# Row-wise L1 normalisation of 16,384 rows: all transfers on SyncE's one queue, in runs of two stores and two loads

## The chip, the core and the metric

The kernel runs on one core of a Trainium2 chip. The time is the device time of one execution in microseconds. Before the change it is 316.64 us (median of 3 runs, 316.48 to 316.65). One further execution was recorded by the hardware profiler. Everything that is said below about single instructions, transfers and packets comes from that execution.

Names used: DVE is VectorE, ACT is ScalarE, SP is SyncE, POOL is GpSimd. "ACTq" and "SPq" are the sequencers of ACT and SP, which issue transfers and wait for semaphores. A transfer is carried out by the core's 16 DMA engines, which are not the same thing as the engines that issue it.

## What is computed

```python
x = np.random.randn(32, 512, 1024).astype(np.float32)
sums = np.sum(np.abs(x), axis=-1, keepdims=True)
out  = (x / (sums + 1e-8)).astype(np.float32)
```

There are 16,384 independent rows of 1,024 fp32 numbers, 4 KB each. Every row is divided by the sum of its absolute values. Input and output are 67.11 MB each, so 134.22 MB have to be moved between HBM and SBUF, and each byte takes part in only two passes over it.

## The kernel before

**Tiling.** A tile is 128 partitions by up to 12 rows of 1,024 numbers, 6,144 KB in all, 49,152 bytes in each partition. There are 128 rows for each partition, cut into eleven tiles: tiles 0 to 9 have 12 rows, tile 10 has 8 (32,768 bytes in each partition). Within a tile each partition holds consecutive rows of HBM, so what one partition loads or stores of a whole tile is one contiguous piece of HBM. Four buffers of a tile's size (`BUFS = 4`) are used in turn: tile i+4 is loaded into the buffer of tile i, and can be loaded only when the store of tile i has landed.

**Compute of one tile** (`normalize`, lines 45 to 73). DVE reduces the whole tile to one sum of absolute values per row (L47, 12.95 us for 12 rows), adds the small constant (L54), takes the reciprocal (L56), and multiplies rows in place by their reciprocal in one broadcast multiply (L58, 12.96 us for 12 rows). For the first three and the last two tiles a few rows are taken from that multiply: `kt` rows are multiplied one by one on DVE (L65, 749 ns a row), `ks` rows on ACT (L68, 1,138 ns a row). The dictionary `split` holds the pairs (kt, ks).

**Order.** The order of instructions is written out by hand in a plain loop: first the loads of tiles 0 to 3, then for every tile its compute, its store, and the load of the tile four further on.

**Queues.** Loads are issued by SP (L87), stores by ACT (L97). So there are two DMA queues, and while both have work the 16 DMA engines serve them side by side: q1 in the profile carries the loads, q10 the stores. ACT also runs the L68 rows, in program order with the stores.

**Packets.** The argument `max_dma_last_dim` cuts what each partition moves into pieces of at most that many bytes, and each piece becomes one packet of the DMA engines. Loads of tiles 0 and 1 and stores of tiles 9 and 10 go whole, one packet per partition. All other loads, and the stores of tiles 1 to 8, go in pieces of 24,576 bytes (16,384 for the load of tile 10), two per partition. The store of tile 0 goes as two transfers, three rows in pieces of 4,096 bytes and nine rows whole; the store of tile 8 goes as two transfers of six rows. That makes 11 loads and 13 stores.

Of the kernel before, what the change touches and what calls it, by code (L numbers as in the profile page):

```python
# [1 line left out]

# [4 lines left out]

FP32 = mybir.dt.float32
EPS = 1e-8


@with_exitstack
def kernel(
    ctx: ExitStack,
    tc: tile.TileContext,
    x: bass.AP,
    out: bass.AP,
):
    nc = tc.nc
    P = nc.NUM_PARTITIONS  # L20

    x_flat = x.flatten_outer_dims()
    out_flat = out.flatten_outer_dims()
    n, d = x_flat.shape

    R = 12
    BUFS = 4
    HEAD = 32
    per_partition = n // P
    assert n % P == 0 and (per_partition - HEAD) % R == 0  # L30
    rows = [R] * ((per_partition - HEAD) // R + 2) + [HEAD - 2 * R]

    def piece(flat, i):
        head = flat[: P * HEAD, :].rearrange("(p r) d -> p r d", p=P)
        if i < 2:
            return head[:, R * i : R * (i + 1), :]
        if i == len(rows) - 1:
            return head[:, 2 * R :, :]
        a = P * (HEAD + R * (i - 2))
        return flat[a : a + P * R, :].rearrange("(p r) d -> p r d", p=P)  # L40

    sbuf = ctx.enter_context(tc.tile_pool(name="sbuf", bufs=BUFS))
    stats = ctx.enter_context(tc.tile_pool(name="stats", bufs=len(rows)))

    def normalize(x_tile, k, kv, kt):
        s = stats.tile([P, R], FP32)
        nc.vector.tensor_reduce(  # L47
            out=s[:, :k],
            in_=x_tile[:, :k, :],
            axis=mybir.AxisListType.X,  # L50
            op=mybir.AluOpType.add,
            apply_absolute_value=True,
        )
        nc.vector.tensor_scalar_add(out=s[:, :k], in0=s[:, :k], scalar1=EPS)  # L54
        inv = stats.tile([P, R], FP32)
        nc.vector.reciprocal(out=inv[:, :k], in_=s[:, :k])  # L56
        if kv:
            nc.vector.tensor_mul(  # L58
                out=x_tile[:, :kv, :],
                in0=x_tile[:, :kv, :],  # L60
                in1=inv[:, :kv].unsqueeze(2).to_broadcast([P, kv, d]),
            )
        for r in range(kv, kv + kt):
            row = x_tile[:, r, :]
            nc.vector.tensor_scalar_mul(out=row, in0=row, scalar1=inv[:, r : r + 1])  # L65
        for r in range(kv + kt, k):
            row = x_tile[:, r, :]
            nc.scalar.activation(  # L68
                out=row,
                in_=row,  # L70
                func=mybir.ActivationFunctionType.Copy,
                scale=inv[:, r : r + 1],
            )

    last = len(rows) - 1
    split = {0: (3, 4), 1: (0, 3), 2: (0, 3), last - 1: (0, 2), last: (4, 4)}

    tiles = {}

    HALF, WHOLE = 24576, 49152
    FIRST = 3

    def load(i):
        x_tile = tiles[i] = sbuf.tile([P, R, d], FP32, name="x_tile")
        nc.sync.dma_start(out=x_tile[:, : rows[i], :], in_=piece(x_flat, i), max_dma_last_dim=WHOLE if i < 2 else HALF)  # L87

    def store(i):
        if i == 0:  # L90
            parts = [(0, FIRST, 4 * d), (FIRST, R, WHOLE)]
        elif i == last - 2:
            parts = [(0, R // 2, HALF), (R // 2, R, HALF)]
        else:
            parts = [(0, rows[i], WHOLE if i >= last - 1 else HALF)]
        for a, b, size in parts:
            nc.scalar.dma_start(  # L97
                out=piece(out_flat, i)[:, a:b, :],
                in_=tiles[i][:, a:b, :],
                max_dma_last_dim=size,  # L100
            )

    def compute(i):
        k = rows[i]
        kt, ks = split.get(i, (0, 0))
        normalize(tiles[i], k, k - kt - ks, kt)

    with tc.manual_schedule():
        for i in range(BUFS):
            load(i)  # L110
        for i in range(len(rows)):
            compute(i)
            store(i)
            if i + BUFS < len(rows):
                load(i + BUFS)


# [1 line left out]
_INS = ['x']  # L119
_OUTS = [((32, 512, 1024), 'float32')]  # L120


# [23 lines left out]
```

## Time and profile before

| quantity | value |
|---|---|
| median time | 316.64 us |
| time of the profiled execution | 316.77 us |
| its span, first to last instruction | 315.2 us |
| DVE busy | 260.6 us (83% of the span) |
| ACT busy | 18.5 us (6%) |
| data moved | 134.22 MB, 426 GB/s over the span |
| DMA packets | 5,761, of which 385 are under 512 bytes |
| share of the 16 DMA engines' time: loads (q1), stores (q10) | 49.8%, 49.4% |

The span is shorter than the time by 1.57 us, which lies around the program's own instructions. The shares of the two queues are the summed durations of their packets, divided by 16 engines times the span. Of the packets under 512 bytes, 384 are the semaphore updates with which each of 24 transfers tells, once per DMA engine, that it has landed. TensorE has no part in this kernel.

In the profile, the idle time of DVE is 29.8 us, all of it ended by a load's landing: 17.8 us before the first tile, the rest in five waits of 1.4 to 2.7 us between 138 and 256 us.

### The profile page before, as it was taken

The numbers are of one execution on the slowest core, as the hardware profiler recorded it, in microseconds if no ns is written. First come the engines' busy times: TensorE is split into PE (matmuls) and PEld (weight loads), VectorE is DVE, ScalarE is ACT, GpSimd is POOL, SyncE is SP. The second block draws the span as 40 slices with busy tenths as digits, with TensorE's granted clock in tenths as the row PEclk, the third lists the DMA queues.
The fourth block names the chain that finished last, engine by engine and source line by source line (L and its number), as shares of the span: only waits on it lengthen the run. The fifth ranks groups of instructions, "written<-read, shape, count | busy, mean of one in ns | idle before, by whom it ended". The sixth has DMA issues, their size and how long they took to land.

```text
span 315.2 us, 172 instructions
## 1 busy us (share of the span) xinstructions
DVE 260.6 (83%) x50; ACT 18.5 (6%) x17; POOL 0.2 (0%) x4
## 2 busy tenths in 40 slices
DVE  0079999999999999989996997999699969999000
ACT  0010503004000000000000000000000000203200
POOL 0000000000000000000000000000000000000000
DMA  8999999999999999999999999999999999999997
GB/s 318 480 399 412 437 407 464 411 436 413 415 446 437 415 446 437 415 449 434 415 449 437 412 449 437 412 449 437 415 446 437 415 437 434 432 428 496 399 408 324
DMA packets 5761, 134.22 MB, mean 426 GB/s; under 512 B 385, under 2 KB 385, under 8 KB 769
## 3 DMA queue, kind: packets, MB, share of 16 engines
q1 hardware_dynamic: 2736, 67.11, 49.8%
q10 hardware_dynamic: 3024, 67.11, 49.4%
q14 instruction: 1, 0.00, 0.0%
HBM read 67.11 MB, written 67.11 MB: 426 GB/s over the span
## 4 chain that ended last, share of the span: by engine, by line
DVE 40%; DMA 33%; another core or an unknown queue 18%; ACT 1%; issue 0%; SPq 0%
DVE s L47 23%; DMA x_tile<-in_x_dram 17%; DMA out_dram<-x_tile 16%; DVE x_tile L58 15%; ACT x_tile L68 1%; DVE x_tile L65 1%; DVE inv L56 0%; DVE s L54 0%; SPq L87 0%
## 5 line engine op out<-in xcount | busy, mean ns | idle before, releaser
L47 DVE TENSOR_REDUCE s<-x_tile 128x12 f32<-128x12288 f32 (+1 forms) x11 | 138.2, 12562 | 29.8 <-DMA x_tile<-in_x_dram 29.8
L58 DVE TENSOR_TENSOR x_tile<-x_tile,inv 128x12288 f32<-128x12288 f32 (+3 forms) x10 | 113.6, 11358 | 0.5
L68 ACT ACTIVATE x_tile<-x_tile,inv 128x1024 f32<-128x1024 f32 x16 | 17.2, 1138 | 256.9 <-DVE inv L56 256.9
L65 DVE TENSOR_SCALAR x_tile<-x_tile,inv 128x1024 f32<-128x1024 f32 x7 | 4.8, 749 | 0.0
L56 DVE RECIPROCAL inv<-s 128x12 f32<-128x12 f32 (+1 forms) x11 | 2.5, 226 | 0.4
L68 ACT ACT_TABLE_LOAD x1 | 1.3, 1283 | 17.8 <-DMA x_tile<-in_x_dram 17.8
L54 DVE TENSOR_SCALAR s<-s 128x12 f32<-128x12 f32 (+1 forms) x11 | 1.9, 174 | 0.4
L130 POOL MEMSET const-bfloat16-1.0<- 128x1 bf16 x1 | 0.1, 101 | 0.0
L130 POOL MEMSET const-uint8-127<- 128x1 uint8 x1 | 0.1, 101 | 0.0
L130 POOL MEMSET const-float32-0.0<- 128x1 f32 x1 | 0.1, 98 | 0.2 <-issue 0.2
L130 POOL MEMSET const-float32-1.0<- 128x1 f32 x1 | 0.1, 98 | 0.0
## 6 DMA issues: line engine op xcount, KB each, us to landing
x_tile<-in_x_dram SPq DMA_DIRECT2D x10, 6144.0 KB, 36.9
out_dram<-x_tile ACTq DMA_DIRECT2D x8, 6144.0 KB, 49.1
out_dram<-x_tile ACTq DMA_DIRECT2D x2, 3072.0 KB, 33.4
out_dram<-x_tile ACTq DMA_DIRECT2D x1, 4608.0 KB, 37.9
x_tile<-in_x_dram SPq DMA_DIRECT2D x1, 4096.0 KB, 32.2
out_dram<-x_tile ACTq DMA_DIRECT2D x1, 4096.0 KB, 20.9
out_dram<-x_tile ACTq DMA_DIRECT2D x1, 1536.0 KB, 29.3
```

What stands on the lines that cost most here:

```text
L47: nc.vector.tensor_reduce(out=s[:, :k], in_=x_tile[:, :k, :], axis=mybir.AxisListType.X, op=mybir.AluOpType.add, apply_absolute_value=True,)
L54: nc.vector.tensor_scalar_add(out=s[:, :k], in0=s[:, :k], scalar1=EPS)
L56: nc.vector.reciprocal(out=inv[:, :k], in_=s[:, :k])
L58: nc.vector.tensor_mul(out=x_tile[:, :kv, :], in0=x_tile[:, :kv, :], in1=inv[:, :kv].unsqueeze(2).to_broadcast([P, kv, d]),)
L65: nc.vector.tensor_scalar_mul(out=row, in0=row, scalar1=inv[:, r : r + 1])
L68: nc.scalar.activation(out=row, in_=row, func=mybir.ActivationFunctionType.Copy, scale=inv[:, r : r + 1],)
L130: nc = _bacc.Bacc("TRN2", target_bir_lowering=False, num_devices=1)
```

## The change

All transfers are issued by SP, each as one transfer per tile without a limit on the piece: one packet of 49,152 bytes per partition for a 12-row tile, one of 32,768 bytes for the 8-row tile. The order on SP's queue becomes: loads 0 to 3; then stores 0 and 1, loads 4 and 5; stores 2 and 3, loads 6 and 7; stores 4 and 5, loads 8 and 9; stores 6 and 7, load 10; stores 8 and 9; store 10. There are 22 transfers in place of 24. ACT keeps the L68 rows and issues no transfer. The division of tile 10's rows changes from (4, 4) to (5, 3): five rows one by one on DVE, three on ACT. The tiles, the four buffers and the work on DVE are otherwise the same.

```diff
-    split = {0: (3, 4), 1: (0, 3), 2: (0, 3), last - 1: (0, 2), last: (4, 4)}
+    split = {0: (3, 4), 1: (0, 3), 2: (0, 3), last - 1: (0, 2), last: (5, 3)}
...
-    HALF, WHOLE = 24576, 49152
-    FIRST = 3
-
     def load(i):
         x_tile = tiles[i] = sbuf.tile([P, R, d], FP32, name="x_tile")
-        nc.sync.dma_start(out=x_tile[:, : rows[i], :], in_=piece(x_flat, i), max_dma_last_dim=WHOLE if i < 2 else HALF)
+        nc.sync.dma_start(out=x_tile[:, : rows[i], :], in_=piece(x_flat, i))
 
     def store(i):
-        if i == 0:
-            parts = [(0, FIRST, 4 * d), (FIRST, R, WHOLE)]
-        elif i == last - 2:
-            parts = [(0, R // 2, HALF), (R // 2, R, HALF)]
-        else:
-            parts = [(0, rows[i], WHOLE if i >= last - 1 else HALF)]
-        for a, b, size in parts:
-            nc.scalar.dma_start(
-                out=piece(out_flat, i)[:, a:b, :],
-                in_=tiles[i][:, a:b, :],
-                max_dma_last_dim=size,
-            )
+        nc.sync.dma_start(out=piece(out_flat, i), in_=tiles[i][:, : rows[i], :])
...
+    RUN = 2
     with tc.manual_schedule():
         for i in range(BUFS):
             load(i)
-        for i in range(len(rows)):
-            compute(i)
-            store(i)
-            if i + BUFS < len(rows):
-                load(i + BUFS)
+        for first in range(0, len(rows), RUN):
+            run = range(first, min(first + RUN, len(rows)))
+            for i in run:
+                compute(i)
+                store(i)
+            for i in run:
+                if i + BUFS < len(rows):
+                    load(i + BUFS)
```

## The prediction

> **What bounds the kernel now.** I read the page's busy shares and its 40 slices first, then the DMA queues, the chain of waits, the transfers' times to landing, and last the packets in chosen stretches. Busy shares, slices and queues:
>
> ```profile
> DVE 260.6 (83%) x50; ACT 18.5 (6%) x17; POOL 0.2 (0%) x4
> DVE  0079999999999999989996997999699969999000
> DMA  8999999999999999999999999999999999999997
> q1 hardware_dynamic: 2736, 67.11, 49.8%
> q10 hardware_dynamic: 3024, 67.11, 49.4%
> ```
>
> The 16 DMA engines are busy in every slice, DVE is not: it starts late, ends early and has dips. The two queues' shares add to 99.2% of 315.2 us, that is 312.7 us of packet time on each engine. So the end is set by the summed packet time, and idle time can be gained only at the two ends, about 2.5 us. The chain of waits, in its middle part:
>
> ```profile
> 111.34 48.94 DMA out_dram<-x_tile
> 160.28 0.02 issue
> ...
> 160.35 0.37 SPq L87
> 160.72 28.68 another core or an unknown queue
> 189.41 0.02 issue
> ...
> 189.48 0.37 SPq L87
> 189.84 28.59 another core or an unknown queue
> 218.43 0.02 issue
> ```
>
> The reader is to see the period. A store lands at 160.28, 189.41 and 218.43, and each landing frees a buffer for the next load: 29.08 us on average for one load and one store of a 12-row tile. Is that the speed of the DMA engines, or do the two directions hinder each other? Three stretches answer it; the columns of the queue lines are packets, MB, and share of 16 engines.
>
> Loads alone with 49,152-byte packets (3 to 31 us):
>
> ```profile
> q1 hardware_dynamic: 256, 11.80, 97.3%
> ```
>
> Loads and stores together with 24,576-byte packets (140 to 230 us):
>
> ```profile
> q1 hardware_dynamic: 841, 19.49, 50.3%
> q10 hardware_dynamic: 839, 19.44, 50.1%
> ```
>
> Stores alone with 32,768-byte packets (305 to 313 us):
>
> ```profile
> q10 hardware_dynamic: 105, 3.44, 99.5%
> ```
>
> In the first, 16 of the 256 are semaphore updates, so 240 packets took 0.973 x 28 x 16 = 435.9 us, or 1.816 us each. Each DMA engine carries 8 partitions, so a 12-row tile takes 8 x 1.816 = 14.5 us one way; two of them are 29.06 us, against 29.08 in the mixture. The third gives 0.995 x 8 x 16 / 105 = 1.213 us. The packet records themselves, sorted by size, have medians of 912 ns for 24,576 bytes, 1,815 for 49,152 and 1,213 for 32,768 in either direction, 609 for 16,384, 1,364 for 36,864 and 159 for 4,096. So each packet has some 9 ns that don't go with its bytes (2 x 912 - 1,815), neither direction is slower than the other, and mixing them costs next to nothing.
>
> **The change part by part.**
>
> *Packets.* On each DMA engine eight loads (tiles 2 to 9) and seven stores (1 to 7) go from 16 packets to 8, the 8-row load from 16 to 8, and the two halves of store 8, 16 together, become 8. That is 8 x (8 + 7 + 1 + 1) = 136 packets fewer. At 9 ns each this is 1.2 us. Store 0 now takes 8 x (3 x 159 + 1,364) ns = 14.73 us, whole 8 x 1,815 = 14.52: 0.2 us. Two transfers fewer save two semaphore updates of 9 ns, nothing. Sum: 1.4 us less packet time on each engine. The whole sum again, as a check: 20 transfers x 8 x 1.815 + 2 x 8 x 1.213 = 309.8 us, plus 22 updates (0.2) and the slow first packet (2.85 in place of 1.815, 1.04) = 311.0, against 312.7 before: 1.7 less, with 0.3 of rounding in the two shares. I take 1.4, the sum over single edits; the landings walked through below, last one at 312.7 against 314.2 before, give 1.5.
>
> *One queue, and SP's waits.* On SP a store now waits for compute, and every load behind it waits with it; a load waits for the landing of the store that frees its buffer, and the stores behind it wait too. None of this costs anything while the queue already holds undone transfers when the next one is issued. A dry queue has a price in the trace: the first load lands 17.0 us after its issue, 2.5 us over its 14.5 of data.
>
> ```profile
> x_tile<-in_x_dram SPq DMA_DIRECT2D x1, 6144.0 KB, 17.0
> ```
>
> So I walk through the order, first load landing at 17.8, then 14.5 us per 12-row transfer and 9.7 for the 8-row ones. Landings: L1 32.3, L2 46.8, L3 61.3, S0 75.8, S1 90.3, L4 104.8, L5 119.3, S2 133.8, S3 148.3, L6 162.8, L7 177.3, S4 191.8, S5 206.3, L8 220.8, L9 235.3, S6 249.8, S7 264.3, L10 274.0, S8 288.5, S9 303.0, S10 312.7. DVE's pass over a full tile is 12.95 (sum) + 0.2 + 0.3 + 12.96 = 26.3 us with gaps; with the splits 20.9 for tile 0, 23.1 for tiles 1 and 2, 24.3 for tile 9. The 8-row tile takes 8.69 + 0.4 + five L65 rows of 0.749 = 12.9 (three L68 rows of 1.138 end before that). The rows:
>
> ```profile
> L47 DVE TENSOR_REDUCE s<-x_tile 128x12 f32<-128x12288 f32 x10 | 129.5, 12949 | 29.8 <-DMA x_tile<-in_x_dram 29.8
> L58 DVE TENSOR_TENSOR x_tile<-x_tile,inv 128x12288 f32<-128x12288 f32 x6 | 77.8, 12959 | 0.4
> L47 DVE TENSOR_REDUCE s<-x_tile 128x8 f32<-128x8192 f32 x1 | 8.7, 8686 | 0.0
> L65 DVE TENSOR_SCALAR x_tile<-x_tile,inv 128x1024 f32<-128x1024 f32 x7 | 4.8, 749 | 0.0
> ```
>
> Compute then ends at 38.7, 61.8, 84.9, 111.2, 137.6, 163.9, 190.3, 216.6 for tiles 0 to 7 without a gap on DVE (each load has landed by then), 247.1 for tile 8 (3.7 us of waiting for L8, in place of the five waits before), 271.4 for tile 9 and 286.9 for tile 10 (waiting for L10, 274.0). Now each issue against the time at which the queue would run dry: S0 38.8 against 60.9; S1 61.9 against 75.4; L4 at S0's landing, 75.9, against 89.9; L5 90.4 against 104.4; S2 90.8 and S3 111.3 against 119 and 133; S4 after L7, 148.8, against 177; S5 164 against 191; S6 after L9, 206.8, against 235; S7 216.7 against 249; L10 249.9 against 264; S8 250.3 against 274; S9 271.5 against 288; S10 287.0 against 302.6. The cover is never under 13 us, nearly one transfer. The waits cost 0. If the cover went, each dry place would cost about 2.5 us. SP's issue of a store (0.34 to 0.50 us on ACTq, loads 0.37) lies under the same cover.
>
> A rule of the Trainium skill speaks against so strict an order (page "DMA: Bandwidth & Descriptors", section "Anatomy of one DMA"): each transfer carries a fixed cost of about 2.0 us besides its bytes, fitted on the other, software path. If a queue paid it for each of 22 transfers, 44 us would be added. By the trace's rows it is paid at the front of the first transfer alone: L1 (issued 1.15, 31.2 us to landing) lands 14.5 us after L0, which is packet time and nothing else.
>
> *Change of direction within one queue.* The order has nine: L3 to S0, S1 to L4, and so on. The trace shows none inside one queue. Low end 0: in the mixture each engine alternates direction at every packet, between the queues, and two tiles took 29.08 us against 29.06. High end: what the very first packet had over the others, 1.04 us each, 9.4 in all. Below nothing is excluded by the one-way stretches, which run at the same packet times. I take 0, the alternating row being nearest.
>
> *ACT, compute, the (5, 3) split.* Stores no longer stand between ACT's rows, and tile 10 ends at 286.9 with 15 us of cover. 0. Before the change the last store was issued at 293.25 with the store ahead of it landing at 304.5, so it was covered too.
>
> *Sum.* 316.77 - 1.4 = 315.4 us for a profiled execution. The median of the runs shown stands 0.13 under it, so 316.64 - 1.4 = 315.2.
>
> **The rivals.**
>
> *A, the same time.* The 9 ns may not be on the path: the summed packet time is 312.7 us, but packets ran from 1.7 to 313.8, 312.1 us, so neighbours overlap by some 4 ns, and if packets of two queues overlap better than those of one, the gain goes. For it: the mixture's 29.08 is under its own 32 x 0.912 = 29.18. Against: one-way stretches overlap alike. Then 316.6 to 316.1.
>
> *B, slower: direction changes stall the one queue.* An engine that must finish a load's writes before it starts a store's reads would lose up to 1.04 us nine times: 316.64 - 1.4 + 9.4 = 324.6. It cancels the gain at 0.16 us a change and shows as slower from 0.22 us on ((1.4 + 0.63) / 9). Against it: the alternation at every packet that costs nothing. For it: that alternation was between two queues with state of their own.
>
> *C, the queue runs dry* behind SP's waits, say at S1, the nearest: 315.2 + 2.5 = 317.7 for each place. It needs an issue 13 us later than worked out.
>
> **How the numbers follow.** What the measurement can tell from no change is about 0.2%, 0.63 us. Chances: forecast 0.79 (315.2, within 314.7 to 315.9: rounding of 0.3 and the two workings, 1.4 and 1.7); A 0.10; B 0.08; C 0.03. Faster takes the forecast's 0.79, same A's 0.10, slower B and C, 0.11. The range 314.7 to 316.6 holds the forecast and A and leaves out B and C and the tails.
>
> **What would show it.** One queue with all 134.22 MB, 3,169 packets (2,816 of data, 352 updates, one of instructions), a share near 99% of the span; span near 313.8; the DMA row at 9 throughout; loads and stores in pairs, a landing every 14.5 us; DVE's waits one near 217 us of some 4 us and one near 271 of 2 to 3. B would show as landings over 14.5 us at each change of direction; C as a slice of the DMA row under 9; A as a sum of packet times that falls by 1.4 while the last landing doesn't move.

## The result, and the profile after

The changed kernel takes 318.97 us (median of 4 runs, 318.12 to 319.20) against 316.62 before: 1.007 times the time, with a 95% interval of 1.0051 to 1.0089. It is slower by 2.35 us where 1.4 us of gain were forecast, and lies outside the forecast range of 314.7 to 316.6. The profiled execution is the fastest of the four, 318.12 us with a span of 316.5, so its account below explains 1.35 us of the 2.35; the other executions have no trace.

The page of the changed kernel, busy shares, slices and the one queue:

```profile
span 316.5 us, 159 instructions
...
DVE 260.9 (82%) x51; ACT 17.4 (6%) x16; POOL 0.2 (0%) x4
...
DVE  0079999999999999999999999994899999595000
...
DMA  8999999899999999999999999999999999999995
...
q1 hardware_dynamic: 3168, 134.22, 98.7%
```

Most of this is as predicted. One queue carries everything, the DMA row stays at 9 but for the first slice, which was an 8 before too, one 8 near 58 us and the 5 at the end, and DVE is not the bound. The chain of waits shows that SP's waits are where they were expected and that the queue wasn't dry:

```profile
164.14 43.74 DMA out_dram<-x_tile
207.89 0.02 issue
207.90 0.34 SPq L82
208.24 0.05 issue
208.30 43.78 DMA out_dram<-x_tile
252.07 0.02 issue
252.09 24.57 DMA x_tile<-in_x_dram
```

Store 5, issued at 164.14, lands 43.7 us later: load 7, store 4 and store 5 itself take 14.5 us each. The walk through the order had that landing at 206.3; it is 207.9. Load 10 lands at 276.7 against 274.0. So the landings drift away from the forecast by 0.9 us at load 3, 1.6 by store 5, 2.7 at the end. Where does a queue that is never dry lose time? In the packets. These are the queue lines of three stretches of the changed kernel: 115 to 117.3 us (the last load packets but one of load 5), 58.5 to 59.2 (the last packets of load 3, store 0 follows), 117.3 to 118.2 (the last packets of load 5, store 2 follows). Columns: packets, MB, share of 16 engines.

```profile
q1 hardware_dynamic: 16, 0.79, 78.9%
...
q1 hardware_dynamic: 16, 0.79, 405.8%
...
q1 hardware_dynamic: 16, 0.79, 218.8%
```

A packet is counted where it starts, so the shares go over 100%; the mean packet is share x stretch, as 16 packets meet 16 engines. That gives 0.789 x 2.3 = 1.815 us, the normal packet; 4.058 x 0.7 = 2.84 us, 1.03 us too long; and 2.188 x 0.9 = 1.97 us, 0.15 too long. Sorted by time, the packet records show all lengthened packets of any size beside a change of direction: the last load packets ahead of stores (1.03, 0.15, 0.03, 0.23 and 0.06 us on average over the engines at the five such changes) and the first two load packets behind stores (up to 0.07). Store packets are not lengthened (by 0.007 us at most). With the program's slow first packets (0.6) the extra time is 2.33 us on average, against 1.46 before.

The average is not all. Extra time falls on the engines unevenly, and a transfer has landed only when all 16 have done their part. The DMA rows of two kernels from 311 to 316 us, in slices of 0.125 us, with each packet counted where it starts; before, then after:

```profile
DMA  9966000099999000000000000000000000000010
```

```profile
DMA  9606069996660606690000600000000000000000
```

Before, the engines start their packets in rounds some 0.5 us wide. After, no round can be seen any more: the last updates of store 10 come between 312.99 and 315.07. The 16 update packets of each transfer tell how this grew: 0.6 us from first to last at load 0, 0.7 at store 0, 1.0 at load 6, 1.6 at load 9, 2.1 at load 10 and from there to the end.

The sum for the profiled pair, from packet records: the mean end of the 16 engines goes from 313.50 to 313.64, which is 0.87 us more of lengthened packets and 0.73 less of everything else, mainly the fewer packets; the last engine is 1.43 us behind that mean in place of 0.33, 1.10 more. Together 1.24 us, against 1.3 in the span.

### The profile page after: what moved, and what is told of

Its sections match the earlier page's. It is cut to its first block, busy times and chain, and to the rows that moved or that the text cites. A ratio compares the mean times of both kernels' runs of the same rounds, so it can differ in the third digit from the quotient of the medians.

```text
span 316.5 us, 159 instructions
## 1 busy us (share of the span) xinstructions
DVE 260.9 (82%) x51; ACT 17.4 (6%) x16; POOL 0.2 (0%) x4
## 4 chain that ended last, share of the span: by engine, by line
DVE 50%; DMA 41%; issue 0%; DVEq 0%; SPq 0%
DMA out_dram<-x_tile 28%; DVE s L47 27%; DVE x_tile L58 20%; DMA x_tile<-in_x_dram 13%; DVE x_tile L65 1%; DVE inv L56 1%; DVE s L54 0%; DVEq L129 0%; SPq L82 0%; DVEq L58 0%
## 5 line engine op out<-in xcount | busy, mean ns | idle before, releaser
L68 ACT ACTIVATE x_tile<-x_tile,inv 128x1024 f32<-128x1024 f32 x15 | 16.1, 1138 | 253.8 <-DVE inv L56 253.8
L65 DVE TENSOR_SCALAR x_tile<-x_tile,inv 128x1024 f32<-128x1024 f32 x8 | 5.5, 749 | 0.0
```

The lines of the kernel that those rows point to most:

```text
L68: nc.scalar.activation(out=row, in_=row, func=mybir.ActivationFunctionType.Copy, scale=inv[:, r : r + 1],)
```

## The experiments

The theory after the comparison (theory 1): on one queue each change of direction lengthens load packets, unevenly, and nothing brings the engines together again. Rivals: the whole packets are at fault; compute traffic in SBUF is; a single queue as such is. The first four runs take the change apart. The runs were made on several chips. The kernel before ran beside each of them (316.57 to 316.63 us); the changed kernel was not repeated, so a difference of a few tenths from its 318.97 shows little.

**Stores back on ACT's queue**, all else as changed.

```diff
-        nc.sync.dma_start(out=piece(out_flat, i), in_=tiles[i][:, : rows[i], :])
+        nc.scalar.dma_start(out=piece(out_flat, i), in_=tiles[i][:, : rows[i], :])
```

> The changed kernel with its stores issued by ACT again, so that loads and stores lie on two queues, all in whole packets. In the changed kernel's profile 1.6 us of mean extra packet time lies on load packets next to a change of direction, and the 16 DMA engines end 2.1 us apart (312.98 to 315.07; before 313.28 to 313.83). Theory 1 (on one queue, a change of direction stalls the load packet beside it): with two queues the stalls go, the packet saving of 1.4 us shows, 315.0 to 315.6 us. Theory 2 (whole packets are at fault, whatever the queue): 318 to 319 us, as the changed kernel.

317.16 us, 1.0016 of before (1.0008 to 1.0025). In this form, one queue against two is worth 1.81 us. But theory 1 had the stalls go with two queues, and the largest did not. This is the queue line of the loads for 40.2 to 41 us, when the first store, issued at 38.73, begins:

```profile
q1 hardware_dynamic: 16, 0.79, 331.1%
```

3.311 x 0.8 = 2.65 us a packet, 0.83 too long. From 40 to 50 us the load packets lose 1.27 us on average, no less than at the first change on one queue (1.03). So the large loss at the first store isn't a price of the single queue. Later losses are smaller with two queues, 0.25 us in all in place of 0.67. And the engines stay nearer to each other: in the two profiled executions (317.28 against 318.12 us) the mean end of the engines is 0.17 us earlier with two queues, and the last engine is 0.76 us behind that mean in place of 1.43. Most of the difference is drift. The 315.2 was not reached either: the other edits don't gain the 1.4 us, they lose 0.5.

**Pieces of 24,576 bytes on the one queue.**

```diff
-        nc.sync.dma_start(out=x_tile[:, : rows[i], :], in_=piece(x_flat, i))
+        nc.sync.dma_start(out=x_tile[:, : rows[i], :], in_=piece(x_flat, i), max_dma_last_dim=24576)
```

and the same for the store.

> The changed kernel, one queue and its order kept, with pieces of 24,576 bytes (16,384 for the 8-row tile), two packets per partition. Theory 1 (direction changes on one queue): the stalls stay and 160 more packets of 9 ns on each engine add 1.4 us to 318.97, 320 to 320.6. Theory 2 (whole packets at fault): the packet time comes back but the stalls go, 316.4 to 317.

319.36 us (1.0067 to 1.0091 of before): theory 2 falls, halves don't mend the queue. They are 0.4 us slower than whole packets here, less than the 1.4 expected (the halves make 176 more packets on each engine, not 160), and the two sets of executions overlap (318.28 to 319.74 against 318.12 to 319.20). The last load packets ahead of store 0 lose only 0.24 us here, and still the engines end 3.1 us apart.

**One store and one load in turn**, 15 changes of direction.

```diff
-        for first in range(0, len(rows), RUN):
...
+        for i in range(len(rows)):
+            compute(i)
+            store(i)
+            if i >= 1 and i - 1 + BUFS < len(rows):
+                load(i - 1 + BUFS)
```

> The changed kernel with one store and one load in turn in place of two and two (after stores 0 and 1), so that the queue changes direction 15 times in place of 9. The queue stays filled by the same working as in the prediction. The changed kernel stands 3.8 us over the forecast of 315.2. Theory 1 with equal stalls at each change: 3.8 x 15 / 9 = 6.3, about 321.5. Theory 1b (most of it lies in the first change, 1.0 us there against 0.06 to 0.25 mean at the later ones): 319 to 320. If changes of direction do not matter: 319.0.

320.53 us (1.0108 to 1.0134): 1.56 more for 6 more changes, 0.26 each. In packet time the changes are not equal; the first is the dearest (0.80 us at load 3's last packets). The engines end 3.5 us apart.

**No compute.**

```diff
-                compute(i)
```

> The changed kernel without compute: the call of it is left out, so that x is copied to the output by the same transfers in the same order on the one queue. Theory 1 (direction changes stall the queue): as the changed kernel, 318.5 to 319.2, stalls at the same places. Theory 3 (DVE's and ACT's traffic in SBUF slows the load packets that it meets): the stalls go, 315 to 315.6.

319.41 us (1.0078 to 1.0104), no faster than with compute, and its packets are lengthened at the same places (0.84 us at load 3's last packets). DVE and ACT have no part in it; theory 3 falls.

The next four look at the form of the stores and at the single change.

**The packet edit alone**, in the kernel before.

```diff
-    HALF, WHOLE = 24576, 49152
+    HALF, WHOLE = 49152, 49152
```

> The kernel before with whole packets for all loads and for stores 1 to 7; two queues, the form of stores 0 and 8 and the order stay. By the spacing of consecutive packets in the records (908.5 ns for 24,576 bytes, 1,811.5 for 49,152: 5.5 ns a packet and not 9) 128 fewer packets on each engine are worth 0.7 us: 315.9. If whole packets cost more where loads meet the first stores (1.3 us of extra packet time at 40 to 45 us with two queues and whole packets, against 0.1 there and 0.6 at 62 us before): 316.6 to 317.2, as the two-queue form of the changed kernel.

Neither: 319.36 us (1.0046 to 1.0107), and far more variable than any other kernel here. Mean extra packet time is low (1.6 us with the start), but from 100 us on it falls on one to three engines at a time, and the distance between the engines grows from 0.6 to 2.8 us. So two queues can lose their step too.

**All loads, then all stores**, without compute, on one queue.

```diff
-        nc.sync.dma_start(out=piece(out_flat, i), in_=tiles[i][:, : rows[i], :])
+        nc.sync.dma_start(out=piece(out_flat, i), in_=tiles[7 + i % 3][:, : rows[i], :])
...
-        for i in range(BUFS):
+        for i in range(len(rows)):
             load(i)
-        for first in range(0, len(rows), RUN):
...
+        for i in range(len(rows)):
+            store(i)
```

> One queue, whole packets, no compute, and one change of direction: all eleven loads, then all eleven stores, which take their data from tiles 7 to 9 (so the output is not the quotient and the waits of loads on stores are gone). Compare with the copy in the changed kernel's order, 319.41 with 9 changes, whose load packets carry 2.2 us of extra time on average beside changes of direction and whose engines' ends lie 2.5 us after their mean. Theory 1 (each change of direction costs): only the first change's 0.8 us and a spread of 0.5 stay, 315.7 to 316.6. If the single queue itself is slow: 319.4.

316.11 us (0.9975 to 0.9992 of before), against 319.41 with nine changes and the same packets: 3.3 us for eight changes, 0.41 each. The single queue as such is not slow. Its share and its last microseconds (311 to 316 us) show it, though here no load waits for a store:

```profile
q1 hardware_dynamic: 3168, 134.22, 99.1%
```

```profile
DMA  0099996000000000000000000000000000000000
```

The last packets start within five slices, and the update packets of a transfer stay 0.6 us apart from the first transfer to the last. The one change costs 0.54 us on average, on the last two load packets of each engine.

**A small early store.**

```diff
+    seeds = ctx.enter_context(tc.tile_pool(name="seeds", bufs=1))
...
+        seed = seeds.tile([P, 128], FP32, name="seed")
+        nc.vector.memset(seed, 0.0)
+        nc.scalar.dma_start(out=piece(out_flat, 0)[:, 0, :128], in_=seed)
         for i in range(BUFS):
```

> The changed kernel with one small store of zeros (512 bytes per partition, into row 0 of each partition's output, later overwritten by store 0) issued by ACT at the very start. Theory 1c (the 1.0 us at the change from load 3 to store 0 is the cost of the program's first store, whenever it comes): that stall falls to the 0.05 to 0.25 us of later changes, about 318.2. Theory 1d (it belongs to that change of direction in the full queue): it stays, 319.0 to 319.3.

320.26 us (1.0097 to 1.0130). The lengthened packets at load 3's end stay, 0.79 us, so a small store at the start does not take that price on itself; whether a large one would was not tried. Why it is 1.3 us slower than the changed kernel was not found; its engines end 2.9 us apart.

**Store 0 in small pieces first**, on the one queue.

```diff
-        nc.sync.dma_start(out=piece(out_flat, i), in_=tiles[i][:, : rows[i], :])
+        parts = [(0, 3, 4 * d), (3, R, 49152)] if i == 0 else [(0, rows[i], 49152)]
+        for u, v, size in parts:
+            nc.sync.dma_start(
+                out=piece(out_flat, i)[:, u:v, :], in_=tiles[i][:, u:v, :], max_dma_last_dim=size
+            )
```

> The changed kernel on its one queue, with store 0 in the form that it has in the kernel before: three rows in pieces of 4,096 bytes, nine rows whole. The pieces cost 0.2 us. Before, with that form, load packets beside the first stores lost 0.1 us near 40 us. Theory 1e (short first packets soften the first change): the 1.0 us at 58 us goes to 0.1 to 0.3, 318.3. If the form of the first store does not matter on one queue: 319.2.

319.93 us (1.0097 to 1.0126), with 0.93 us still at load 3's end: on one queue the form of the first store doesn't help. Theory 1e falls.

The last four ask what at a change costs, and close the account.

**Every change behind an empty queue**, without compute. The loop is written out over four fixed buffers, so that the first transfer after a change uses the buffer of the last one before it.

```diff
...
+        slots = {k: sbuf.tile([P, R, d], FP32, name="x_tile") for k in "ABCD"}
+        for i, key in enumerate("BCAD"):
+            load_into(i, key)
+        for first in range(0, len(rows), 2):
+            run = list(range(first, min(first + 2, len(rows))))
+            todo = [i + BUFS for i in run if i + BUFS < len(rows)]
+            for i, key in zip(run, "AD" if first == 8 else "DA"):
+                store_from(i, key)
+            for i, key in zip(todo, "AD" if len(todo) == 2 else "A"):
+                load_into(i, key)
```

> The copy without compute in the changed kernel's order of loads and stores on one queue, with the buffers assigned so that the first transfer after each of the nine changes of direction uses the buffer of the last transfer before it, and so waits for its landing (the output is a permuted copy). The queue runs dry at each change, and no DMA engine can load while another one stores. The price is 9 times landing plus issue, about 1.9 us each (0.6 to 0.9 from the last packet to the landing, 1.0 from issue to the first packet), 17 us: about 333 us. Theory 2a (the extra time of load packets comes from engines that load while others already store, or the reverse): no load packet beside a change is lengthened beyond the start-up that follows a dry queue, and the 16 engines stay within 0.7 us of each other to the end. Theory 2b (each engine pays for its own change of direction): the lengthened load packets stay, 0.1 to 1.0 us at the last load packet before the stores.

335.07 us (1.0571 to 1.0598). The queue line for 58.3 to 60.5 us, load 3's last packets with two semaphore updates, and for 92.7 to 93.7 us, load 4's first packets:

```profile
q1 hardware_dynamic: 18, 0.79, 82.6%
...
q1 hardware_dynamic: 16, 0.79, 262.7%
```

0.826 x 2.2 = 1.82 us a packet: with the queue drained, the last load packets are as long as any other, at all five changes to stores, where the filled queue gave 2.65 in the same copy. The first load packets after a drain are long, 2.63 us, much like the program's very first ones (0.7 us extra). And the update packets, up to 1.7 us apart during loads, are back to 0.2 at each store. So theory 2b, in the form stated, falls: a change costs the last load packet nothing when all is quiet. But a drained engine has its time to finish before the store comes, so this doesn't tell whether an engine in a filled queue waits for its own writes. Theory 2a is not shown either. In the changed kernel the earliest engine's last load packet was lengthened too: it ran for 3.09 us from 58.57, where 1.815 would have ended it at 60.4, and the first store packet of any engine started at 61.20. What a filled queue does to a load packet just ahead of stores, and whether its own engine or others do it, stays open.

**Both edits undone that concern queue and pieces**, with stores 0 and 8 in one transfer.

```diff
-        nc.sync.dma_start(out=x_tile[:, : rows[i], :], in_=piece(x_flat, i))
+        nc.sync.dma_start(out=x_tile[:, : rows[i], :], in_=piece(x_flat, i), max_dma_last_dim=24576)
...
-        nc.sync.dma_start(out=piece(out_flat, i), in_=tiles[i][:, : rows[i], :])
+        nc.scalar.dma_start(out=piece(out_flat, i), in_=tiles[i][:, : rows[i], :], max_dma_last_dim=24576)
```

> The changed kernel with both edits undone that concern the DMA engines: stores on ACT's queue, pieces of 24,576 bytes. Left of the change are store 0 and store 8 as one transfer each and (5, 3). With it the four combinations stand: one queue whole 318.97, one queue halves 319.36, two queues whole 317.16. If two queues with halves keep the engines in step, as in the kernel before: 316.4 to 316.8. If packets only count by their number: 317.9.

317.10 us (1.0007 to 1.0025), between the two forecasts. The engines stay in step, 0.5 us apart from first to last landing. It differs from the kernel before in more than its expectation names: besides stores 0 and 8 and (5, 3), loads 0 and 1 and stores 9 and 10, which went whole there, are in halves here. That is 32 more packets on each engine, an estimated 0.18 us at 5.5 ns each (the spacing of packets in the expectation of "The packet edit alone"). The rest is largely seen at the first store. The queue lines for 40.6 to 41.2 us, here and before:

```profile
q1 hardware_dynamic: 16, 0.39, 224.9%
```

```profile
q1 hardware_dynamic: 16, 0.39, 153.5%
q10 hardware_dynamic: 14, 0.06, 23.2%
```

And before at 62.2 to 62.7 us, the last load packets but one of load 3:

```profile
q1 hardware_dynamic: 16, 0.39, 269.9%
```

The load packets beside store 0 take 2.249 x 0.6 = 1.35 us here and 0.92 before, where that store begins with 4,096-byte pieces (normal: 0.91). But the kernel before pays later: at 62 us its load packets take 2.699 x 0.5 = 1.35 us too, where here they are normal. In all the load packets of that time lose 0.96 us here and 0.68 before. So the small pieces, which cost 0.2 us by their number, save about 0.3. Stores 0 and 8 in one transfer, with (5, 3) and the four halved transfers, come to 0.5 us more; the parts of store 8 and of (5, 3) were not taken apart.

**Whole packets in the kernel before, store 0 whole too.**

```diff
-    HALF, WHOLE = 24576, 49152
+    HALF, WHOLE = 49152, 49152
...
-        if i == 0:
-            parts = [(0, FIRST, 4 * d), (FIRST, R, WHOLE)]
-        elif i == last - 2:
+        if i == last - 2:
```

> The kernel before with whole packets everywhere, store 0 in one transfer too; store 8 in two halves and (4, 4) stay. The version with store 0 in small pieces first took 319.36 (316.52 to 321.54) with engines 2.8 us apart at the end; the two-queue form of the changed kernel, with stores 0 and 8 in one transfer, 317.16 with engines 1.25 us apart. If the form of store 0 sets how the two queues' packets meet: 317.2 here. If it is store 8 or the (4, 4): 319.4.

317.65 us (1.0021 to 1.0045), nearer to 317.2 than to 319.4, with engines 1.3 us apart at the end. With whole packets on two queues, then, store 0 in one transfer is the better form by 1.7 us, the opposite of what the rows with halves showed, though the executions of the two overlap (316.76 to 318.30 against 316.52 to 321.54). Why the engines drift in the one and not in the other stays open.

**Runs of three**, 7 changes of direction.

```diff
-    RUN = 2
+    RUN = 3
```

> The changed kernel with three stores and three loads in turn (RUN = 3): 7 changes of direction in place of 9, each store and load still issued before the queue is dry by the same working (the nearest are store 2, store 8 and store 10, with 5, 5 and 1.4 us of cover). From 9 to 15 changes the time went from 318.97 to 320.53, 0.26 us a change. If the count of changes sets the loss: about 318.4. If it does not, 319.0; if a store comes late after all, 2 us more for each dry place, visible as a slice of the DMA row under 9.

318.42 us (1.0048 to 1.0076), where the count of changes has it. But its executions (317.55 to 318.98) overlap with those of nine changes (318.12 to 319.20), so the two aren't told apart. And in the profiled execution, the fastest, the queue ran dry once: store 10 was issued at 303.32, when the first engines had ended store 9 at 303.2, and engines stood idle for up to 1.3 us. That brought them together, from 1.7 us apart to 0.6. The engine that ended last had no gap, so this execution was not made longer by it.

The times by number of changes on one queue: 316.11 (1, copy only), 318.42 (7), 318.97 (9; copy 319.41), 320.53 (15). One against nine is clear. But with nine changes a small early store gave 320.26 and small pieces in store 0 gave 319.93, so the count is not all that sets the time, and a price for each change is rough. And by queue and packet, with stores 0 and 8 in one transfer:

| | one queue | two queues |
|---|---|---|
| whole packets | 318.97 | 317.16 |
| halves | 319.36 | 317.10 |

From before to after, one step at a time: 316.62, then 317.10 (stores 0 and 8 in one transfer, (5, 3), four transfers halved: 0.5 more), 317.16 (whole packets: 0.1 more), 318.97 (one queue: 1.8 more). These steps hold in this order. With store 0 in small pieces first, whole packets alone cost 2.8 us (319.36), and the version with one queue took 319.93, which is hardly told apart from it.

## Why the prediction was wrong

- *What bounds the kernel* was right: packet time on the DMA engines sets the end in every version that keeps its queue filled, and the copy without compute was no faster.
- *SP's waits and the cover* were right. The queue was never dry; DVE waited before tiles 8 and 10 as said, 5.5 and 3.5 us in place of 3.7 (4.2 by the walk's own 216.6 and 220.8) and 2.6, because the landings were late. The price of a dry place, put at 2.5 us, was (335.07 - 316.11) / 9 = 2.1. The page "DMA: Bandwidth & Descriptors" of the Trainium skill, section "Anatomy of one DMA", has about 2.0 us for a transfer's fixed cost, on another path; these runs agree where the queue is empty.
- *Change of direction within one queue, "I take 0"*, is the step that failed. The row it went by was not near enough: in the mixture the alternation is between two queues that are both filled, and there, once under way, it is indeed free. On one queue nine changes cost 1.8 us against two queues, 0.20 each, and 0.26 to 0.41 by the other two counts, inside the bounds of 0 and 1.04. Rival B, at a chance of 0.08, had the kernel slower, and it is. Whether its mechanism is the right one stays open: a drained change costs the last load packet nothing, and the largest stall, at the first store, comes with two queues as well. And most of the loss in the profiled pair, 1.10 of 1.24 us, is the engines' drift, which no part of the prediction had.
- *Packets, 1.4 us*, was mis-sized. 9 ns was the difference of recorded durations, but neighbouring packets overlap by 3.5 ns in the records; from start to start it is 5.5 ns, and the profiled pair gained some 0.73 with store 0's part in it. So rival A was half right. On two queues the time didn't move at all (317.10 to 317.16): with whole packets the engines end 1.3 us apart in place of 0.5, which takes the gain. So of the 3.8 us over the forecast 1.8 belong to the one queue, and 2.0 to packets and store forms, which were put at 1.4 of gain and cost 0.5.
- *Store 0, 0.2 us of gain*, was priced by the pieces' own time alone and not by what they do to the loads beside them. That goes both ways: on one queue the small pieces made the kernel 1.0 us slower (319.93 against 318.97), with whole packets on two queues 1.7 slower (319.36 against 317.65); with halves on two queues the rows beside the first store show them saving about 0.3.

## What to carry to other kernels

Where the DMA engines are always busy, look for lengthened packets and for the distance between first and last engine of a landing, not only for dry queues: a transfer is as late as its last engine, and in these runs engines that were out of step on one queue came together to any extent only when it ran dry. Where one queue carries both directions, change direction seldom (316.11 us with one change, 319.41 with nine). Two queues were 1.8 us faster here, with store 0 in one transfer; with small pieces in front of whole packets they drifted as well, so look at the engines' distance there too. A rate measured in steady one-way stretches says nothing of the places where the direction changes.

## What the runs showed that was not expected

- One queue against two, with the same packets and store 0 in one transfer, cost 1.8 us (whole) and 2.3 us (halves). The Trainium skill, page "DMA: Bandwidth & Descriptors", section "Rules for kernel authors", says that spreading transfers over issuing engines doesn't help bandwidth, as all run on the same 16 DMA engines. Here the steady rates agree with that (1.815 us a packet either way), the total doesn't.
- Only load packets are lengthened to any size: at the start, at the first store whether there are one or two queues, and at later changes of direction. Store packets keep their time to a few hundredths, but for three in "The packet edit alone" (up to 0.18 us).
- At later changes the engines that are behind bear more of it: in the changed kernel the eight engines that began the transfer later lost 0.29 us on the last two packets of load 9 and 0.12 on those of load 10, the eight earlier ones 0.18 and 0.005. At the first change it was the other way round (0.89 and 1.16).
- Whole packets in the kernel before gave 316.5 to 321.5 us from one execution to the next, the kernel before 316.4 to 317.0.
